# Output projection of a hybrid decoder step: classical blocks against Strassen's seven products

## The chip, the cores and the metric

The kernel runs on one core of one Trainium2 chip. The metric is device time in microseconds (us) for one execution of the whole step; less is better. Three timed runs of the kernel before gave 1225.06, 1226.51 and 1226.95 us. Engines are named as in the profile: PE (matrix multiply), PEld (its weight load), DVE (vector), ACT (scalar), POOL (GpSimd), SP (issues the DMAs).

## The reference

One layer: x <- x + W_out [mLSTM ; GDN], then a final RMSNorm. 1040 prompt tokens (16 meta tokens, whose outputs are dropped, and 1024 real ones) and 8 sample tokens share the weights.

```python
u = _rms_norm(x, norm_w) @ w_in                       # 1048 x 1024 @ 1024 x 8216
ym = (_head_rms(hm).reshape(bsz, t, M_V) * w_mnorm * sigmoid(o_m) * silu(z_m))
yg = (_head_rms(og) * w_gnorm).reshape(bsz, t, G_V) * silu(z_g)
y = jnp.concatenate([ym, yg], axis=-1) @ w_out        # 1032 x 2048 @ 2048 x 1024
x = x + y
y_prompt = _rms_norm(xp[:, META:], final_norm_w)
```

The change concerns the last product, `y @ w_out`, with the residual and the final norm behind it. All data are f32. A product of f32 precision is made of three matmuls in the type fp32r: each operand a is split into a high part h (ACT's copy to fp32r) and a low part l = a - h (a subtraction on DVE), and h*H + l*H + h*L are summed in PSUM.

## The kernel before, in words

**Input projection.** 65 weight tiles of 128 output columns (a gate tile, 24 GDN tiles, 16 mLSTM tiles, 24 gate-path tiles) are multiplied one after another; most are jobs of 72 matmuls (3 token blocks of up to 350 columns, 8 tiles of K, 3 terms). Feature-major: the weight tile stands still, tokens move. A job's raw weights are loaded two jobs ahead by SP into one of two buffers `wr`, split by ACT and DVE during the job before. The recurrences of the 8 GDN heads and the 4 mLSTM heads, and the 8 samples, are woven between these matmuls.

**Gates.** `gate(kt, wcol)` makes one of 16 tiles y (128 features x 1024 tokens): it loads the head output `ht` from DRAM, scales it on POOL, turns it with 8 PE transposes (`hT`), multiplies it with the gate on DVE. kt 8..15 are the GDN half of K, kt 0..7 the mLSTM half. mLSTM gates follow the last 16 jobs (`o0, zm0, ... o7, zm7`) one pair at a time. Of each y the first 256 tokens are split in SBUF, the other 768 are written to DRAM (`y_d`).

**Output projection.** Three token blocks of 256, 512 and 264 columns (`OUT`; the 8 samples ride in the last). For each block, each of 8 output tiles f and each half of K, 24 matmuls (8 K tiles, 3 terms) with the weight tile standing still: 3 x 8 x 2 x 24 = 1152 matmuls. Each half tile of weights (512 KB) is loaded, split and used once per block, so 48 loads. `finish` copies a PSUM tile to SBUF on ACT, turns it back to token-major with PE transposes (`otr`), and adds it to the residual rows `xr` on DVE; squares, mean and scaling follow per block.

**What sets the order.** The kernel is one generator program run by `Plan`, which keeps a clock for each engine and emits instructions thread by thread; `filler` is the thread of the projections, and all others (`chains`, `gates`, `finish`, loads) are stepped in between when the plan thinks their inputs are there. The order in each engine's queue is fixed by this at build time. SP's queue is in order too: a DMA whose wait is not met holds back all behind it.

Of the kernel before, what the change touches and what calls it, by code (L numbers as in the profile page):

```python
# [20 lines left out]
P = 128  # L21
D = 1024
# [42 lines left out]
class Plan:  # L65
# [9 lines left out]
    def __init__(self):  # L75
# [5 lines left out]
        self.threads = []  # L81

    def note(self, eng, op, out, ins, extra, power):
# [4 lines left out]
        if op == "dma_start":  # L88
            load = getattr(out.tensor, "space", DRAM) != DRAM
            start = max([self.clock[eng], self.read.get(out.tensor.name, 0.0), self.dmas[-self.QUEUED]] + [self.done.get(x.tensor.name, (0.0, ""))[0] for x in ins])  # L90
# [7 lines left out]
            self.done[out.tensor.name] = self.dmas[-1], "dma"  # L98
            return
        start = self.clock[eng]  # L100
        for x in ins:
            t, e = self.done.get(x.tensor.name, (0.0, eng))
            if e != eng:
                start = max(start, t + self.LAT)
            elif eng == "pool" or self.place.get(x.tensor.name) == x.offset:
                start = max(start, t + self.SELF[eng])
        for x in (*ins, out):
            t, e = self.last.get(x.tensor.name, (0.0, eng))
            if e != eng:
                start = max(start, t + self.LAT)  # L110
        ptr = sum(free(x) == 1 for x in ins[1:])
        if eng == "pe":
# [7 lines left out]
            else:  # L120
                cost = 1e-3 * m + (0.0 if self.tiled else 0.32)
# [16 lines left out]
        for x in ins:  # L138
            self.read[x.tensor.name] = start + cost
        for x in (*ins, out):  # L140
            if x.tensor.name in self.psum:
                self.last[x.tensor.name] = start + cost, eng
        for x in (out, extra):
            if x is not None:
                self.done[x.tensor.name] = start + cost, eng
                self.place[x.tensor.name] = x.offset

    def shares(self, op, out, ins):

        if any(x.tensor.name in self.psum for x in (*ins, out)):  # L150
# [3 lines left out]
    def when(self, x, wait):  # L154
        t, e = self.done.get(x.tensor.name, (0.0, ""))
        return t + (self.DMA if e == "dma" else wait + self.POOL * (e == "pool"))

    def take(self, tag, bufs, t):

        names, name = self.banks.setdefault(tag, [""] * bufs), t.tensor.name  # L160
# [21 lines left out]
    def step(self, t):  # L182
# [5 lines left out]
        if isinstance(x, tuple):  # L188
            t[1] = self.done.get(x[0].tensor.name, (0.0, ""))[0] + x[1]
# [1736 lines left out]
```

## Time and profile before

| | |
|---|---|
| three runs, median (range) | 1226.51 us (1225.06 to 1226.95) |
| the profiled execution, its own time | 1225.61 us |
| its span in the trace | 1223.8 us |
| PE busy | 1208.6 us, 99% |
| DVE, ACT, POOL busy | 794.1, 584.9, 498.9 us |
| output projection on PE, first to last matmul | 1025.3 to 1214.2 us |
| last matmul to the end of the span | 9.6 us |

All instructions go through a recording helper, so every one carries line 56; they are told apart by the tiles they write and read. `op` is the output projection's PSUM tile, `pjzm` that of the last input projection. Matmul durations in the trace overlap (they are pipelined), so a matmul's price is read from the distance between starts.

### The profile page before, as it was taken

What the parts mean: (1) busy time and instruction counts of PE and PEld (TensorE: products, weight loads), DVE (VectorE), ACT (ScalarE), POOL (GpSimd) and SP (SyncE); (2) the same over time, 40 slices, a digit from 0 to 9 for tenths busy, and PEclk for the clock granted to TensorE, in tenths of its full rate; (3) what the DMA queues carried; (4) which work ended last, traced back from release to release, by engine and by line L of the source; (5) the groups of instructions that cost most, each with busy time, mean ns of one, the idle gap of its engine ahead of it and who ended that gap; (6) DMA issues with size and microseconds to landing.
All of it is one profiled execution on the core that took longest, in us unless ns stands there. A gap on an engine that the chain in (4) does not pass through costs nothing.

```text
span 1223.8 us, 23909 instructions
## 1 busy us (share of the span) xinstructions
PE 1208.6 (99%) x8802; PEld 1150.5 (94%) x8802; DVE 794.1 (65%) x2053; ACT 584.9 (48%) x1861; POOL 498.9 (41%) x674
## 2 busy tenths in 40 slices
PE   9999999999999999999999999999999999999997
PEld 7999999999999999999998999999999999988896
DVE  6789786687968688953356556457567644763365
ACT  6544355667465656554544435342222223644344
POOL 3105887818584837682030431434365310000001
PEclk9999999999999999999999999999999999999998
DMA  6032213221312221212132353335687535793362
GB/s 238 18 99 84 79 43 87 81 72 41 87 54 64 66 78 47 67 61 56 31 99 91 136 167 119 130 141 178 234 292 271 185 141 206 257 327 103 97 217 85
DMA packets 83312, 150.80 MB, mean 123 GB/s; under 512 B 26089, under 2 KB 49857, under 8 KB 83194
## 3 DMA queue, kind: packets, MB, share of 16 engines
q1 hardware_dynamic: 83000, 149.10, 36.8%
q8 instruction: 69, 1.13, 0.4%
q14 instruction: 49, 0.40, 0.1%
q10 hardware_dynamic: 194, 0.17, 0.1%
HBM read 113.97 MB, written 35.26 MB: 122 GB/s over the span
## 4 chain that ended last, share of the span: by engine, by line
PE 88%; DVE 6%; issue 4%; ACT 1%; POOL 1%; DVEq 0%; POOLq 0%; ACTq 0%
PE pjg L56 20%; PE op L56 14%; PE pjm L56 12%; PE pjz L56 7%; PE pjzm L56 7%; PE pjo L56 7%; PE up L56 4%; PE tp L56 3%; PE sk L56 2%; PE mnm L56 2%; PE mup L56 1%; PE hT L56 1%; PE kk L56 1%; PE E L56 1%; PE W L56 1%
## 5 line engine op out<-in xcount | busy, mean ns | idle before, releaser
L56 PE MATMUL pjg<-xht,whg 128*128 128x350 f32 (+6 forms) x624 | 197.7, 324 | 1.0 <-ACT xht L56 1.0
L56 PE MATMUL pjg<-xlt,whg 128*128 128x350 f32 (+6 forms) x624 | 197.1, 323 | 0.0
L56 PE MATMUL pjg<-xht,wlg 128*128 128x350 f32 (+6 forms) x592 | 191.2, 326 | 0.0
L56 POOL TENSOR_TENSOR tmp<-B,E 33x31 f32<-33x31 f32 (+15 forms) x248 | 146.8, 592 | 74.8 <-DMA B<-nd 56.0
L56 PE MATMUL op<-y,who 128*128 128x256 f32 (+2 forms) x768 | 173.3, 319 | 0.0
L56 POOL TENSOR_TENSOR E<-E,tmp 33x31 f32<-33x31 f32 (+15 forms) x248 | 155.4, 627 | 19.4
L56 PEld LDWEIGHTS op<-y,who 128*128 128x128 f32 x768 | 126.9, 188 | 9.5
L56 PE MATMUL pjm<-xht,whm 128*128 128x350 f32 (+2 forms) x384 | 126.6, 330 | 0.0
L56 PE MATMUL pjm<-xht,wlm 128*128 128x350 f32 (+2 forms) x384 | 126.4, 329 | 0.0
L56 PE MATMUL pjm<-xlt,whm 128*128 128x350 f32 (+2 forms) x384 | 125.9, 328 | 0.0
L56 PE MATMUL op<-y,wlo 128*128 128x256 f32 (+2 forms) x384 | 124.3, 324 | 0.1
L56 PEld LDWEIGHTS pjg<-xht,whg 128*128 128x128 f32 x624 | 116.5, 189 | 1.8 <-issue 1.2
L56 PEld LDWEIGHTS pjg<-xlt,whg 128*128 128x128 f32 x624 | 116.4, 189 | 0.5
L56 PEld LDWEIGHTS pjg<-xht,wlg 128*128 128x128 f32 x592 | 111.0, 189 | 0.4
L56 DVE SCALAR_TENSOR_TENSOR kq<-cr,prm,kq 128x346 f32<-128x346 f32 (+7 forms) x147 | 92.5, 633 | 11.5 <-ACT cr L56 5.4
L56 PEld LDWEIGHTS op<-y,wlo 128*128 128x128 f32 x384 | 72.2, 188 | 5.2 <-DVE wlo L56 0.3
L56 PEld LDWEIGHTS pjm<-xht,wlm 128*128 128x128 f32 x384 | 72.5, 189 | 1.0 <-issue 0.4
L56 PEld LDWEIGHTS pjm<-xht,whm 128*128 128x128 f32 x384 | 72.4, 188 | 0.6 <-issue 0.4
L56 PEld LDWEIGHTS pjm<-xlt,whm 128*128 128x128 f32 x384 | 72.3, 188 | 0.3 <-issue 0.2
L56 DVE TENSOR_TENSOR wlo<-wro,who 128x384 fp32r<-128x384 f32 (+1 forms) x90 | 41.5, 508 | 36.8 <-ACT who L56 36.8
L56 PE MATMUL pjz<-xlt,whz 128*128 128x344 f32 x192 | 62.8, 327 | 0.0
L56 POOL TENSOR_TENSOR fst<-fst,mhalf 128x1 f32<-128x1 f32 (+1 forms) x9 | 5.0, 580 | 141.5 <-DVE fst L56 141.5
(319 smaller groups left out, 3171.9 us busy)
## 6 DMA issues: line engine op xcount, KB each, us to landing
wrg<-in_wt SPq DMA_DIRECT2D x23, 512.0 KB
ebuf<-in_wo SPq DMA_DIRECT2D x22, 512.0 KB
wro<-in_wo SPq DMA_DIRECT2D x22, 512.0 KB
wrm<-in_wt SPq DMA_DIRECT2D x16, 512.0 KB
ht<-h_d SPq DMA_DIRECT2D x16, 512.0 KB
y_d<-y SPq DMA_DIRECT2D x16, 384.0 KB
yr<-y_d SPq DMA_DIRECT2D x12, 512.0 KB
gm<-rows_d SPq DMA_DIRECT2D x8, 576.0 KB
```

What stands on the lines that cost most here:

```text
L56: r = f(*args, **kw)
```

## The change

The output projection is computed as Strassen's product of 2 x 2 blocks. The left matrix y is cut into token halves (512 tokens) and K halves (GDN first, mLSTM second); W_out into the same K halves and two halves of 512 output columns. Seven block products (`PRODUCTS`) take the place of eight; each is 4 token tiles x 8 K tiles x 3 terms = 96 matmuls of 512 columns, 672 in all. Now the token tile stands still (128 x 128 of the left block) and 512 weight columns move, so the result is token-major and is added to the residual rows directly from PSUM (`drain`), without copy and without transposes.

- **Left blocks.** The first product's left block (GDN, first tokens) is split in SBUF by the gates (`slot`). Second-half minus first-half (`s_d`), the mLSTM second half and four sums or differences (`c_d`) are formed by POOL in the gates and written to DRAM: 1 subtraction of 512 per GDN gate, an addition of 1024 and two operations of 512 per mLSTM gate, which also reads the GDN tile back from `y_d`. For products 1..6 each of the 8 left tiles is loaded over its own used low part (`left_loads`), and split by ACT and DVE (`left_splits`).
- **Right blocks.** The 16 raw weight pieces (2 K tiles x 512 columns, 512 KB) are loaded once and stay: in `ebuf`, in `wr`, and in 12 places of the memory of x, which is free when the input projection has ended (`places`, `weight_loads`). Five products need a sum or difference of two pieces: 20 POOL operations of 128 x 1024 (`right_sums`). 28 right operands are split into two buffers in turn (`right_splits`): operand n needs the matmuls of operand n - 2 done.
- **Samples.** 32 f32 matmuls against the raw weights: 32 columns (8 samples and neighbours) stand still, in four column groups of the array in turn, 512 weight columns move (`sample_rows`).
- Square sums and scaling are taken per token tile, when the last product that touches a half row has been drained.

PE's order where the last input job ends, before (`pjzm` <- `xht`, `xlt`: last job; `who`, `wlo`: high and low part of a weight tile; `hT`: the last gate):

```order
L56 MATMUL pjzm_2_12936<-xlt,whzm_12813 128x344
L56 MATMUL pjzm_2_12936<-xht,wlzm_12814 128x344
L56 MATMUL op_0_12975<-y_8_10675,who_0_1_12909 128x256 x2
L56 MATMUL op_0_12975<-y_8_10675,wlo_0_1_12910 128x256
...
L56 MATMUL op_0_12975<-y_12_11745,who_0_1_12909 128x256 x2
L56 MATMUL hT_0_13004<-ident,ht_12760 128x128 x4
L56 MATMUL hT_1_13010<-ident,ht_12760 128x128 x4
```

and in the change (`owh`, `owl`: a right operand; `left`: high and low left tiles; `op_0` to `op_3`: the four token tiles):

```order
L56 MATMUL pjzm_2_12986<-xlt,whzm_12837 128x344
L56 MATMUL pjzm_2_12986<-xht,wlzm_12838 128x344
L56 MATMUL op_0_13031<-owh_12914,left_10758 128x512
L56 MATMUL op_0_13031<-owl_12915,left_10758 128x512
L56 MATMUL op_0_13031<-owh_12914,left_10758 128x512
L56 MATMUL op_1_13032<-owh_12914,left_10758 128x512
L56 MATMUL op_1_13032<-owl_12915,left_10758 128x512
L56 MATMUL op_1_13032<-owh_12914,left_10758 128x512
L56 MATMUL hT_0_13041<-ident,ht_12880 128x128 x4
L56 MATMUL hT_1_13047<-ident,ht_12880 128x128 x4
```

Both start the output projection right behind the last job, with the last gate's eight transposes inside.

SP's queue from the moment the memory of x is free, in the change (`regionxh`, `regionxl`: weight pieces in the memory of x; `left<-s_d`: left tiles of product 1; `yg`, `c_d`: the last mLSTM gate; `in_x_p`: residual rows):

```order
L56 DMA regionxh<-in_wo 128x1024 x5
L56 DMA left_10758<-s_d 128x512
L56 DMA c_d<-y_12960 128x512
L56 DMA yg_13066<-y_d 128x1024
L56 DMA left_10758<-s_d 128x512
L56 DMA regionxh<-in_wo 128x1024
...
L56 DMA xr_3_13217<-in_x_p 128x1024
L56 DMA xr_3_13219<-in_x_p 128x1024
L56 DMA db<-in_final_w 128x1024
L56 DMA regionxl<-in_wo 128x1024
L56 DMA left_10758<-c_d 128x512 x2
```

From the first row to the last `regionxl<-in_wo` shown stand 30 DMAs: 9 weight pieces, 8 left tiles, 8 residual tiles, the final norm's weights, and 4 of the last gate, 12.75 MiB; that last piece is the first that product 2 needs. Before, the weight loads were spread over the whole projection.

POOL's queue at the same place (`db`, `regionxl` on the left: sums of weight pieces; `ht`, `yg`: left sums of the last two mLSTM gates):

```order
L56 TENSOR_TENSOR db<-wout_12763,wout_12871 128x1024
L56 TENSOR_TENSOR ht_12880<-ht_12880,rs_12882 128x1024
L56 TENSOR_TENSOR ht_12811<-y_12879,yg_12932 128x1024
L56 TENSOR_TENSOR yg_12932<-yg_12932,y_12879 128x512
L56 TENSOR_TENSOR yg_12932<-y_12879 128x512
L56 TENSOR_SCALAR gs<-mg_12920,wmq 128x8
L56 TENSOR_TENSOR regionxl<-regionxh 128x1024 x2
L56 TENSOR_TENSOR regionxl<-regionxh,ebuf_101 128x1024
L56 TENSOR_TENSOR ht_12880<-y_12960,yg_13066 128x1024
```

Before, POOL had only the `ht`, `gs` and `rs` work of the gates here, and nothing but the norms' small operations behind it.

The diff, cut to what the prediction speaks of (left out: the plan's bookkeeping by parts of a tile, the rings' choice of any free buffer, the residual loads, the old loads of y):

```diff
         pool.tensor_scalar(gs[:, kt_, :], g[:, SEQ:NO], wcol, None, op0=ALU.mult)
+        (r_v if kt_ < 8 else r_gm).free(gi)
+        u = ht.rearrange("p c t -> p (c t)")
+        yield y
+        if kt_ >= 8:
+            sp.dma_start(y_d[j], y)
+            high, low = slot(j)
+            act.copy(high, y[:, 0:HALF])
+            pool.tensor_tensor(out=u[:, 0:HALF], in0=y[:, HALF:SEQ], in1=y[:, 0:HALF], op=ALU.subtract)
+            yield high
+            dve.tensor_tensor(out=low, in0=y[:, 0:HALF], in1=high.bitcast(F32), op=ALU.subtract)
+            yield u
+            sp.dma_start(s_d[j], u[:, 0:HALF])
+        else:
+            sp.dma_start(c_d[j, :, 0], y[:, HALF:SEQ])
+            yield r_gm.can
+            gi, g = r_gm.get([SEQ], f"yg{j}")
+            sp.dma_start(g, y_d[j])
+            yield g
+            pool.tensor_tensor(out=u, in0=y, in1=g, op=ALU.add)
+            yield u
+            sp.dma_start(c_d[j, :, 1:3], u.rearrange("p (a t) -> p a t", a=2))
+            pool.tensor_tensor(out=g[:, 0:HALF], in0=g[:, 0:HALF], in1=y[:, HALF:SEQ], op=ALU.add)
+            pool.tensor_tensor(out=g[:, HALF:SEQ], in0=y[:, 0:HALF], in1=y[:, HALF:SEQ], op=ALU.subtract)
+            yield g
+            sp.dma_start(c_d[j, :, 3:5], g.rearrange("p (a t) -> p a t", a=2))
+            r_gm.free(gi)
         r_gm.free(hi)
-        (r_v if kt_ < 8 else r_gm).free(gi)
-        yield y
-        yh_, yl_ = y0[kt_]
-        act.copy(yh_, y[:, 0:NB])
-        yield yh_
-        dve.tensor_tensor(out=yl_, in0=y[:, 0:NB], in1=yh_.bitcast(F32), op=ALU.subtract)
-        yield y
-        sp.dma_start(y_d[kt_], y[:, NB:SEQ])
         r_y.free(yi)
         done.add(("y", kt_))
...
+    PRODUCTS = (
+        (((0, 1), (1, 1), SUB), ((0, 1, ADD), (1, 1, ADD))),
+        (((0, 0), (0, 1), ADD), ((1, 1, ADD),)),
+        (((1, 0), (0, 0), SUB), ((0, 0, ADD), (1, 0, ADD))),
+        (((0, 0), None, None), ((1, 0, ADD), (1, 1, SUB))),
+        (((0, 0), (1, 1), ADD), ((0, 0, ADD), (1, 1, ADD))),
+        (((1, 1), None, None), ((0, 0, SUB), (0, 1, ADD))),
+        (((1, 0), (1, 1), ADD), ((0, 0, ADD),)),
+    )
+    LEFT = (None, (s_d, None), (c_d, 0), (c_d, 2), (c_d, 3), (c_d, 1), (c_d, 4))
+    NP, NI = len(PRODUCTS), 4
...
+    def places():
+
+        yield has("samples")
+        for e in ebuf:
+            yield e.rearrange("p a b -> p (a b)")
+        for i in range(2):
+            yield has("split", i)
+            t = wp.tile([P, 2 * HALF], F32, tag="wr", name=f"wout{i}")
+            plan.read[t.tensor.name] = plan.read.get(wrs[-2], 0.0)
+            wrs.append(t.tensor.name)
+            yield t
         yield has("x")
+        for tag, old in (("xh", xht), ("xl", xlt)):
+            t = xp.tile([P, 32 * 264], F32, tag=tag, name=f"region{tag}")
+            plan.split(t, D, old.tensor.name)
+            region.extend(t[:, D * i : D * i + D] for i in range(8))
+        done.add(("region",))
+        yield from region[0:12]
...
+    def weight_loads():
+
+        where = places()
+        for q in [((r, 1), i) for i in range(NI) for r in range(2)] + [((r, 0), i) for r in range(2) for i in range(NI)]:
+            for t in where:
+                if hasattr(t, "tensor"):
+                    break
+                yield t
+            (r, c), i = q
+            if c == 0:
+                yield has("used", r, 2 * i)
+            raw[q] = t.rearrange("p (k c) -> p k c", k=2)
+            sp.dma_start(raw[q], a["wo"][r, c, i])
+            if len(raw) % 2 == 0:
+                yield None
+        done.add(("raw",))
+
+    def right_sums():
+
+        n = 0
+        for p, ((b1, b2, op), _) in enumerate(PRODUCTS):
+            for i in range(NI):
+                yield lambda: (b1, i) in raw and (b2 is None or (b2, i) in raw)
+                t = raw[b1, i]
+                if b2 is not None:
+                    yield lambda: all(m in right for m in sums if m < n - 1) and (n != 1 or 0 in right)
+                    if n > 1:
+                        yield has("region")
+                    yield raw[b1, i]
+                    yield raw[b2, i]
+                    t = (fwb if n < 2 else region[12 + n % 2]).rearrange("p (k c) -> p k c", k=2)
+                    pool.tensor_tensor(out=t, in0=raw[b1, i], in1=raw[b2, i], op=op)
+                sums[n] = t
+                n += 1
+
+    def right_splits():
+
+        for n in range(NP * NI):
+            yield lambda: n in sums and ("item", n - 2) in done
+            yield sums[n]
+            wh, wl = (wp.tile([P, 2, HALF], F32R, tag=f"w{i}", name=f"ow{i}{n}") for i in "hl")
+            if n > 1:
+                plan.old.update((x.tensor.name, plan.read[o.tensor.name] + plan.LAT) for x, o in zip((wh, wl), right[n - 2]))
+            for k in range(2):
+                act.copy(wh[:, k], sums[n][:, k])
+            for k in range(2):
+                dve.tensor_tensor(out=wl[:, k], in0=sums[n][:, k], in1=wh[:, k].bitcast(F32), op=ALU.subtract)
+            right[n] = wh, wl
+
+    def left_loads():
+        for p in range(1, NP):
+            t, c = LEFT[p]
             for k in range(8):
+                yield lambda: ("used", p - 1, k) in done and (p == 1 or ("y", k) in done)
+                sp.dma_start(slots[k][1].bitcast(F32), t[k] if c is None else t[k, :, c])
+                done.add(("left", p, k))
+
+    def left_splits():
+
+        for p in range(1, NP):
+            for k in range(8):
+                yield has("left", p, k)
+                high, low = slots[k]
+                yield low
+                yield "act"
+                act.copy(high, low.bitcast(F32))
+                yield high
+                yield "dve"
+                dve.tensor_tensor(out=low, in0=low.bitcast(F32), in1=high.bitcast(F32), op=ALU.subtract)
+                done.add(("parts", p, k))
+
+    def out_products():
+
+        for p in range(NP):
+            banks = []
+            for tag in ("pj", "pj", "k", "k") if p % 2 == 0 else "ssss":
+                yield room(tag)
+                banks.append(bank(tag, f"op{p}_{len(banks)}"))
+            done.add(("product", p))
+            steps = [(k, t) for i in range(NI - 1) for k in (2 * i, 2 * i + 1) for t in range(4)] + [(k, t) for t in range(4) for k in (6, 7)]
+            if p == NP - 1:
+                steps = steps[0:16] + [(k, t) for k0 in (4, 6) for t in (0, 1) for k in (k0, k0 + 1)] + [(k, t) for t in (2, 3) for k in range(4, 8)]
+            for k, t in steps:
+                n = NI * p + k // 2
+                yield lambda: n in right
+                wh, wl = right[n]
+                yield wl
+                yield has("parts", p, k) if p else lambda: ("y", 8 + k) in done
+                yield slots[k][1]
+                for x, (l, r) in enumerate(((0, wh), (0, wl), (1, wh))):
+                    pe.matmul(banks[t], slots[k][l][:, P * t : P * t + P], r[:, k % 2], start=k == 0 and x == 0, stop=k == 7 and x == 2)
+                if t == 3:
+                    done.add(("used", p, k))
+                    if k % 2:
+                        done.add(("item", n))
+                if k == 7:
+                    plan.add(drain(p, t, banks[t]))
+                yield None
...
+    def drain(p, t, pt):
+
+        to = PRODUCTS[p][1]
+        yield lambda: all((c, t) in xr for c, _, _ in to) and (p == 0 or ("drain", p - 1, t) in done)
+        for c, h, op in to:
+            x_ = xr[c, t][:, HALF * h : HALF * h + HALF]
+            yield x_
+            dve.tensor_tensor(out=x_, in0=x_, in1=pt, op=op)
+        done.add(("drain", p, t))
+        if p not in (3, 4, 5, 6):
+            return
+        c, h = {3: (1, 0), 4: (1, 1), 5: (0, 1), 6: (0, 0)}[p]
+        x_, last = xr[c, t], p in (4, 6)
+        part = x_[:, HALF * h : HALF * h + HALF]
+        if not last:
+            stats[c, t] = w("fst", [4], f"fst{c}_{t}", 9)
+        st = stats[c, t]
+        yield part
+        act.activation(junk, part, AF.Square, accum_out=st[:, last : last + 1])
+        if not last:
+            yield st
+            dve.tensor_scalar(st[:, 0:1], st[:, 0:1], EPS * D, None, op0=ADD)
+            if p == 5:
+                yield lambda: ("fw",) in done
+                pool.tensor_tensor(out=part, in0=part, in1=fwb[:, HALF * h : HALF * h + HALF], op=ALU.mult)
+            return
+        yield st
+        dve.tensor_scalar(st[:, 2:3], st[:, 1:2], st[:, 0:1], 1.0 / D, op0=ADD, op1=ALU.mult)
+        pool.tensor_tensor(out=st[:, 3:4], in0=st[:, 2:3], in1=mhalf[:, 0:1], op=ALU.pow)
+        yield st
+        if p == 4:
+            yield lambda: ("fw",) in done
+            yield "dve"
+            dve.scalar_tensor_tensor(out=x_, in0=x_, scalar=st[:, 3:4], in1=fwb, op0=ALU.mult, op1=ALU.mult)
+        else:
+            dve.scalar_tensor_tensor(out=part, in0=part, scalar=st[:, 3:4], in1=fwb[:, 0:HALF], op0=ALU.mult, op1=ALU.mult)
+            act.activation(x_[:, HALF:D], x_[:, HALF:D], AF.Copy, scale=st[:, 3:4])
+        q0 = HALF * c + P * t
+        sp.dma_start(o["y_p"][q0 : q0 + P, :], x_)
...
+        for h in range(2):
+            yield room("s")
+            pt = pst(f"ops{h}")
+            for k in range(16):
+                j = k % 4
+                pe.matmul(
+                    pt[32 * j : 32 * j + 32], yf[:, 8 * k : 8 * k + 32], raw[(k < 8, h), k % 8 // 2][:, k % 2],
+                    start=k < 4, stop=k >= 12)
...
-    def finish(blk, f, pt):
...
-            act.copy(oT[:, 0:m_], pt[:, c0 : c0 + m_])
-            tr = pst(f"otr{blk}_{f}_{c0}")
-            for i, m in part:
-                j = P * i - c0
-                pe.transpose(tr[0:m, j : j + P], oT[:, j : j + m], ident)
-            for i, m in part:
-                j, x_ = P * i - c0, xr[blk, i][2]
-                dve.tensor_tensor(out=x_[0:m, fs], in0=x_[0:m, fs], in1=tr[0:m, j : j + P], op=ALU.add)
...
-    def out_products():
-
-        for blk in range(3):
-            seq = [(f, half) for f in range(8) for half in (1, 0)]
-            if blk == 0:
-                seq[0:8] = [(f, 1) for f in range(4)] + [(f, 0) for f in range(4)]
-            for f, half in seq:
-                yield blk, f, half
...
-        "wo": w_out.reshape(2, KT, P, 8, P).transpose(3, 0, 2, 1, 4),
+        "wo": w_out.reshape(2, 4, 2, P, 2, D // 2)[::-1].transpose(0, 4, 1, 3, 2, 5),
```

More of the change, by code (lines that the diff above doesn't have):

```diff
@@ L80, in __init__, with key, split @@
         self.banks, self.dmas = {}, [0.0] * self.QUEUED
-        self.threads = []
+        self.threads, self.parts, self.old = [], {}, {}
+    def key(self, x):
+        name = x.tensor.name
+        if name not in self.parts:
+            return name
+        pitch, size = self.parts[name]
+        return name, x.offset % pitch // size
+    def split(self, t, size, old=None):
+        pitch = t.ap[0][0] if old is not None else 1 << 40
+        self.parts[t.tensor.name] = pitch, size
+        if old:
+            for i in range(pitch // size + 1):
+                self.read[t.tensor.name, i] = self.read.get(old, 0.0)
     def note(self, eng, op, out, ins, extra, power):
@@ new lines, in hymba_kernel, with slot @@
+    s_d = dr.tile([GH, P, HALF], F32, name="s_d")
+    c_d = dr.tile([GH, P, 5, HALF], F32, name="c_d")
+    for t, size in ((y_d, P * SEQ), (s_d, P * HALF), (c_d, 5 * P * HALF)):
+        plan.split(t, size)
+    slots = {}
+    r_y = Ring(plan, lambda i, name: wk.tile([P, SEQ], F32, tag="BE"[i], name=name, bufs=1), 2)
+    def slot(k):
+        if k not in slots:
+            r, n = (r_kq, 2) if k < 6 else (r_N, 1)
+            _, t = r.get([n, 2, HALF], f"left{k}", F32R)
+            plan.split(t, HALF, r.old)
+            for i in range(n):
+                slots[k + i] = t[:, i, 0], t[:, i, 1]
+        return slots[k]
@@ new lines, in hymba_kernel, with residual @@
+    stats = {}
+    def residual():
+        yield has("region")
+        xs_ = region[15][0:NS]
+        for n, (c, t) in enumerate([(c, t) for t in range(4) for c in range(2)]):
+            if c == 0:
+                yield has("used", 0, 4 + t)
+            if n == 0:
+                x_ = region[14]
+            else:
+                r = r_v if n < 5 else r_gm
+                yield lambda: r.can() and (n < 5 or ("y", 7) in done)
+                _, x_ = r.get([D], f"xr{c}_{t}")
+            q0 = HALF * c + P * t
+            sp.dma_start(x_, a["x_p"][q0 : q0 + P, :])
+            xr[c, t] = x_
+        yield lambda: 1 in right
+        sp.dma_start(fwb, a["final_w"].partition_broadcast(P))
+        done.add(("fw",))
+        yield has("raw")
+        sp.dma_start(xs_, a["x_s"])
+        xr["s"] = xs_
```

313 lines of the change are left out of this document (80 added, 233 removed).

## The prediction

> **What bounds the kernel now.** First the page: busy time by engine, the slices, the chain.
>
> ```profile
> PE 1208.6 (99%) x8802; PEld 1150.5 (94%) x8802; DVE 794.1 (65%) x2053; ACT 584.9 (48%) x1861; POOL 498.9 (41%) x674
> ...
> PE   9999999999999999999999999999999999999997
> ...
> PEclk9999999999999999999999999999999999999998
> ...
> PE 88%; DVE 6%; issue 4%; ACT 1%; POOL 1%; DVEq 0%; POOLq 0%; ACTq 0%
> ```
>
> PE has work in every slice but the last, at full granted clock, and is 88% of the chain that ended last. Time is saved only by taking work off PE, or in the tail; everything else counts once it makes PE wait. Next the stretches of the output projection (its three blocks, then the tail; columns: PE, PEld, DVE, ACT, POOL busy us, clock, DMA share, GB/s):
>
> ```profile
> 1025.30:1068.60 43.30, 43.30 (x370) 43.30 (x369) 29.85 (x65) 26.78 (x63) 0.93 (x1) 1.00 0.87 310
> 1068.60:1166.50 97.90, 97.90 (x476) 81.72 (x476) 45.72 (x119) 41.49 (x108) 1.10 (x2) 1.00 0.48 167
> 1166.50:1213.90 47.40, 47.31 (x389) 46.73 (x388) 31.44 (x80) 24.53 (x69) 4.75 (x6) 1.00 0.49 167
> 1213.90:1223.80 9.90, 0.87 (x6) 0.37 (x4) 5.26 (x12) 2.63 (x8) 3.32 (x4) 0.67 0.29 110
> ```
>
> PE is gapless in all three blocks; DVE reaches 69% and POOL is nearly idle. So a cheaper product is worth its full PE time, as long as DVE, POOL and the DMAs keep up.
>
> **What leaves PE, and what comes.** The timeline of PE (start, us, operation; x2: two merged):
>
> ```profile
> 1025.33 0.40 PE L56 MATMUL op<-y,who 128*128 128x256 f32 x2
> ...
> 1027.68 1.04 PE L56 MATMUL hT<-ident,ht 128*128 128x128 f32 x8
> 1028.47 0.37 PE L56 MATMUL op<-y,wlo 128*128 128x256 f32 x1
> ...
> 1102.32 0.62 PE L56 MATMUL op<-y,who 128*128 128x512 f32 x2
> ...
> 1107.76 0.62 PE L56 MATMUL op<-y,who 128*128 128x512 f32 x2
> ...
> 1213.94 0.28 PE L56 MATMUL op<-y,wlo 128*128 128x264 f32 x1
> ```
>
> The old projection takes 1213.94 + 0.28 - 1025.33 = 188.9 us, with its narrow blocks, 72 transposes back and the last gate's hT. A matmul of 512 columns: 24 stand between 1102.32 and 1107.76, 0.2267 us each, at clock 1.00 over the whole middle block. The change has the same shape (128 x 128 stands still, 512 columns of fp32r move): 672 x 0.2267 = 152.3 us. The hT stay: 1028.47 - 1027.68 = 0.8.
>
> The 32 sample matmuls are new. Nearest rows: eight f32 matmuls in four column groups with 128 columns, and single f32 matmuls with 257 columns:
>
> ```profile
> 865.52 0.65 PE L56 MATMUL mqc<-db,msam 128*32 128x128 f32 x16
> 866.10 0.42 PE L56 MATMUL pjzm<-xht,whzm 128*128 128x344 f32 x1
> ...
> 701.66 0.60 PE L56 MATMUL mnm<-C,mwq 128*128 128x257 f32 x2
> 702.10 0.60 PE L56 MATMUL mnm<-va,mpm 128*128 128x257 f32 x2
> ```
>
> A single one costs 0.44 for 257 columns, so 0.88 for 512; 32 one after another 28 us. The eight took 0.58, 0.0725 each, where one alone would be 0.44 / 2 = 0.22: three at a time. By that row 32 x 4 x 0.0725 = 9.3 us; with all four groups busy 28 / 4 = 7. I take 8, between these, since longer streams lose less at the change of groups.
>
> PE: -188.9 + 152.3 + 0.8 + 8 = **-27.8 us**.
>
> **What PE may have to wait for in the steady products.** A block of 24 matmuls (one right operand) lasts 24 x 0.2267 = 5.44 us, a product 21.8. Prices:
>
> ```profile
> L56 DVE TENSOR_TENSOR wlo<-wro,who 128x384 fp32r<-128x384 f32 x44 | 22.6, 554 | 33.6 <-ACT who L56 33.6
> L56 ACT CAST who<-wro 128x384 fp32r<-128x384 f32 x44 | 20.4, 513 | 16.5 <-PE op L56 13.1 <-issue 3.4
> L56 DVE TENSOR_TENSOR y<-yr,y 128x1024 fp32r<-128x1024 f32 x12 | 14.6, 1220 | 3.1 <-ACT y L56 3.1
> L56 ACT CAST y<-yr 128x1024 fp32r<-128x1024 f32 x12 | 12.5, 1046 | 1.2 <-DMA yr<-y_d 1.2
> L56 DVE SCALAR_TENSOR_TENSOR y<-hT,wmq,mg 128x512 f32<-128x512 f32 x2 | 1.4, 747 | 0.0
> L56 POOL TENSOR_TENSOR ebuf<-ebuf,wb 128x1024 f32<-128x1024 f32 x8 | 15.2, 1898 | 23.2 <-DMA ebuf<-mvb_d 23.2
> ```
>
> By interpolation to 512 columns a DVE split is 0.69 and an ACT copy 0.62; a drain from PSUM is at most the 0.75 of the `y<-hT` row; a POOL sum of 1024 is 1.9. A right operand may be split once operand n - 2 has been used, so one block before its own use: ACT 0.62, then DVE 0.69 for the first half, 2 x 0.62 + 0.69 = 1.9 for both, in 5.44. The left tiles have three quarters of a product, 16 us, for load, copy and split. DVE per product: 8 x 0.69 right, 8 x 0.69 left, 8 x 0.75 drains = 17.0 of 21.8 us, 78%; ACT 16 x 0.62 = 9.9; POOL 4 x 1.9 = 7.6. All fit under PE's 21.8; if this cover goes, see the rivals. Bounds for these waits: 0, and 14 (rival A). I take 1, near the zero end, because PE stayed gapless with DVE at 69% in these very blocks.
>
> **What PE may wait for at the start.** Two rows for a load of 512 KB (issued, and first used by POOL), two for the lead of the last jobs' weights:
>
> ```profile
> 977.28 0.33 SPq L56 DMA_DIRECT2D wro<-in_wt  x1
> 1000.64 0.42 SPq L56 DMA_DIRECT2D ht<-h_d  x1
> ...
> 1005.31 1.90 POOL L56 TENSOR_TENSOR ht<-ht,rs 128x1024 f32<-128x1024 f32 x1 [1.27 <-DMA ht<-h_d]
> ...
> 1005.42 8.80 PE pjo L56 x56
> ```
>
> A load is there after 4.7 us; 0.52 MB at the 310 GB/s of the first block are 1.7 of it, so 3.0 is latency. At full DMA share the rate would be 310 / 0.87 = 356. Product 0's third operand needs the first two pieces loaded into x: 4.7 + 1.7, POOL 1.9, ACT 0.62: 8.9 us after x is free, needed after two blocks, 10.9. It holds by 2. Product 2's first operand is tighter: its piece is the last of 12.75 MiB (13.4 MB) in SP's queue. At 310 it lands after 43.1 + 3.0, at 356 after 37.6 + 3.0; with POOL and ACT 48.6 or 43.1. Product 2 begins 2 x 21.8 + 0.8 = 44.3 us after the first. Wait between 0 and 4.3; I take 2. Ahead of that piece in SP's queue stand residual loads and left tiles that wait for PE's use of the old ones; behind it product 2's left tiles.
>
> **Gate stage.** POOL gets 8 x 1.2 + 8 x (1.9 + 2 x 1.2) = 44 us (512 columns at 1.2, between half and two thirds of the 1.9), DMA some 14.7 MB more. Cover:
>
> ```profile
> 800.00:900.00 100.00, 98.76 (x680) 93.55 (x680) 57.57 (x149) 31.73 (x96) 42.15 (x27) 1.00 0.59 198
> 900.00:950.00 50.00, 50.00 (x380) 48.09 (x379) 36.27 (x57) 13.35 (x36) 31.37 (x19) 1.00 0.80 278
> 950.00:1000.00 50.00, 50.00 (x342) 49.49 (x340) 29.19 (x63) 11.35 (x28) 15.31 (x11) 1.00 0.48 162
> 1000.00:1025.00 25.00, 25.00 (x164) 24.98 (x163) 7.75 (x16) 5.29 (x13) 2.21 (x2) 1.00 0.26 83
> ```
>
> POOL is busy 91 of 225 us here, 135 after. The DMAs move 43.9 MB, 58.6 after: 260 GB/s of 356. SP's queue now has DMAs that wait for POOL, ahead of weight loads; but these are issued at 977.28 for a job at 1005.42, 28 us ahead. I count 0; from that cover, a weight load would have to be 15 us late before PE feels it.
>
> **Tail.**
>
> ```profile
> 1211.24 4.16 POOL L56 TENSOR_TENSOR xr<-xr,db 128x896 f32<-128x896 f32 x2 [39.62 <-issue]
> 1211.79 1.58 DVE L56 TENSOR_TENSOR fst<-fst 128x1 f32<-128x1 f32 x1 [0.30 <-ACT wa L56]
> 1213.48 1.94 DVE L56 TENSOR_TENSOR fst<-fst 8x1 f32<-8x1 f32 x1
> 1216.61 1.82 POOL L56 TENSOR_TENSOR fst<-fst,mhalf 128x1 f32<-128x1 f32 x3 [1.20 <-DVE fst L56]
> ...
> 1219.86 0.30 SPq L56 DMA_DIRECT2D out_y_s<-xr  x1
> ...
> L56 ACT ACTIVATE wa<-xr 128x512 f32<-128x512 f32 x8 | 5.1, 632 | 0.8 <-DVE xr L56 0.6
> L56 DVE TENSOR_TENSOR fst<-fst 128x1 f32<-128x1 f32 x8 | 2.7, 333 | 1.1 <-ACT wa L56 1.1
> ```
>
> Now 5.6 us pass from the last matmul to the last output's issue, with copy, transposes, three squares and three powers. After: drain 0.75, square 0.8 (512 columns on ACT, 0.63, and its read-out, put at 0.2), a small DVE step 0.2, power 0.6, scaling 0.7, handovers put at 0.5: 3.5. But the last output is 512 KB instead of 32 KB, 1.4 us at 356. Gain 0 to 2; I take 1.
>
> **Sum.** 1225.6 (the profiled execution) - 27.8 - 1 + 1 + 2 = 1199.8. The median stands 0.9 above that execution: **1201 us**.
>
> **Rivals.**
> *A, DVE becomes the bound by POOL's lock.* In the last fence two DVE additions of single numbers took 1.58 and 1.94 us while POOL ran its two of 2 us; the other seven of the group's eight take (2.7 - 1.58) / 7 = 0.16. So a long POOL operation can hold DVE for its length. If each of the 20 sums does that to a split, a product costs DVE 17.0 + 7.6 = 24.6 against 21.8, +2.8 in five products: 1201 - 1 + 14 = 1214. Against: a third of DVE's time here reads PSUM. (The Trainium skill, page "SBUF — State Buffer", section "SBUF: two separate sides", says that DVE and GpSimd share one port pair under an exclusive lock for a whole instruction, for DVE operations with two SBUF inputs; the row above agrees. By that rule alone the sum would be 1214.)
> *B, the loads at the start.* If SP's waits keep the DMAs below 300 GB/s, at 250 the piece lands after 53.6 + 3 + 2.5: 15 us late. Price 6 to 15 in place of 2: 1205 to 1214.
> *C, slower.* The two-buffer chain of right operands becomes the period: if after operand n - 2's last use DVE first finishes a left pair (1.4), two drains (1.5) and waits out a sum (1.9) before the split (1.9), the chain is 6.7, 1.3 over the block; in all 28 blocks +36: 1201 - 1 + 36 = 1236. It decides from 26 / 28 = 0.95 us of excess per block. Against: that is the whole DVE load of a block, and two operands are in flight.
> *D, the gates.* SP's waits for POOL hold up weight loads; at 1 us per job of the last 16, 1217. For: SP waits in order; against: 28 us of lead.
> That the products are not really fewer is excluded: the order holds 672.
>
> **How the numbers follow.** Forecast 0.62, with its own range 1195 (no wait, samples 7, tail 2) to 1206; A 0.10; B 0.15; C 0.05; D 0.05; the rest 0.03 is faster still. The range of 8 in 10 takes in A, B and D: 1194 to 1217. A measurement of this kernel tells 0.2% (2.5 us) from no change; faster by more than that are all but C, and 0.02 for a mixture of A, B and D that just cancels the gain: 0.93; same 0.02; slower 0.05.
>
> **What would show it.** Right: `op` matmuls 0.227 us apart over some 163 us, PE gapless but for a few us around product 2; no `otr`. Wrong: PE waiting for `owl` or `owh` in every block (A, C), for DMA pieces in products 0 to 2 (B), PE gaps before 1025 (D), or sample matmuls taking 28 us.

## The result, and the profile after

The change made the kernel slower: 1241.56 us median of 4 runs (1237.19 to 1244.01) against 1226.73 for the kernel before (1225.06 to 1227.1), a ratio of 1.012 with a 95% interval of 1.0085 to 1.0154. The forecast was 1201, its range 1194 to 1217. The profiled execution took 1244.01 us, its span is 1241.9.

The page of the changed kernel, busy time, two rows of the slices, and the chain by engine and by line:

```profile
PE 1197.3 (96%) x8314; PEld 1115.5 (90%) x8314; DVE 858.0 (69%) x1964; ACT 560.9 (45%) x1750; POOL 608.5 (49%) x728
...
PE   9999999999999999999999999999898888999996
...
PEclk9999999999999999999999999999899988999999
...
PE 73%; DVE 9%; DMA 8%; issue 5%; POOL 3%; ACT 1%; SPq 1%; POOLq 0%; DVEq 0%; ACTq 0%
PE pjg L56 20%; PE pjm L56 12%; PE op L56 9%; PE pjz L56 7%; PE up L56 4%; PE pjzm L56 4%; PE tp L56 3%; PE pjo L56 3%; DMA c_d<-yg 3%; PE sk L56 2%; DMA ht<-h_d 2%; DVE left L56 2%; PE mnm L56 1%; POOL ht L56 1%; PE mup L56 1%
```

Before, PE was 88% of the chain and no DMA stood in it. Now DMAs are 8% of it, and two are named: the write of `c_d` out of `yg`, and the load of `ht`. PE has holes in five of the slices from 29 to 34, and in three of these five its clock is lower too. Slice 29 begins at 869 us: that is the gate stage, not the projection. The stretches show how much (columns as in the prediction; the stage from 800 us to the first `op` matmul, the projection, the tail), first the kernel before, then the change:

```profile
800.00:1025.30 225.30, 224.06 (x1561) 216.42 (x1561) 130.78 (x282) 61.71 (x173) 91.04 (x58) 1.00 0.58 195
```

```profile
800.00:1059.70 259.70, 234.88 (x1560) 224.82 (x1559) 156.03 (x274) 60.95 (x165) 140.54 (x89) 0.95 0.65 217
...
1059.70:1234.00 174.30, 167.35 (x746) 129.32 (x745) 147.39 (x186) 69.54 (x139) 66.98 (x34) 0.99 0.47 164
1234.00:1242.00 8.00, 0.41 (x2) 0.00 (x0) 2.44 (x5) 2.14 (x4) 1.54 (x2) 0.83 0.64 256
```

Much the same 1560 matmuls take 34.4 us longer before the projection begins. Of these PE is idle for 24.8 - 1.2 = 23.6 (stretch less busy time, of each kernel), and busy for 234.9 - 224.1 = 10.8 more, at a mean clock of 0.95. The projection itself became shorter: from the first `op` matmul at 1059.7 to the end of the last at 1234.4 are 174.7 us, 14.2 less than the 188.9 before. The tail is 7.5 in place of 9.6. Together +34.4 - 14.2 - 2.1 = +18.1, and the two profiled executions differ by 18.4. So the projection's gain is there, if only 14.2 us of the 24.8 forecast (27.8 less 3 of waits), and the gate stage gives back more than all of it.

Who waits in the stage from 800 to 1062, in the groups of waits of the change (total us, times, longest):

```profile
POOL ht L56 <- DMA ht<-h_d: 52.2, 11, 10.3
...
PE hT L56 <- POOL ht L56: 18.0, 7, 5.2
```

These waits for `ht` are 18.0 of PE's 24.8 us of idle time; the largest of the rest are 3.0 for DVE's `wb` and 2.1 for a load of the samples' state. What SP's queue waits for there:

```profile
SPq L56 <- DMA c_d<-yg: 35.6, 6, 7.4
SPq L56 <- DMA s_d<-ht: 34.0, 8, 5.8
SPq L56 <- DVE y L56: 26.7, 8, 7.6
...
SPq L56 <- POOL ht L56: 12.2, 6, 7.5
```

A piece of the chain of waits shows one round of it (start, us, what):

```profile
945.23 7.54 DMA c_d<-yg
...
953.15 5.44 DMA ht<-h_d
...
958.74 1.91 POOL ht L56
...
960.69 0.67 PE hT L56 x4
...
961.39 1.42 DVE y L56 x2
...
962.86 5.47 DMA yg<-y_d
...
968.40 3.00 POOL ht L56
...
971.46 3.71 POOL yg L56 x2
...
978.81 7.87 DMA c_d<-yg
```

A gate's sums are written to DRAM for 7.5 us; only then may the next GDN gate's `gg` be loaded, since it goes into the buffer that the write reads (`r_gm` has three, and `gg`, `ht` and now `yg` all come from it). Its `ht`, which goes into the buffer of the write `c_d<-ht` issued just before, stands behind `gg` in SP's queue. After the load come POOL's scaling, the transposes on PE, `y`, the reading back of the GDN tile into the buffer that `gg` held, the sums, 3.6 us of other work on POOL and SP, and the next write: 33.6 us from one `c_d<-yg` to the next. In the same way the mLSTM gate's `ht` waits for the write `s_d<-ht`. Before the change the buffers came free when PE, DVE and POOL had read them, with no DRAM write in between. PE takes its work in order and meets the transposes (`hT`) before POOL has made `ht`. Other than by the forecast's rival D, no weight load is late: the waits of PE hold none for `who`, `wlo`, `whzm` or `wlzm`.

### The profile page after: what moved, and what is told of

The parts are those of the page before. It is cut to its first block, busy times and chain, and to the rows that moved or that the text cites. A ratio compares the mean times of both kernels' runs of the same rounds, so it can differ in the third digit from the quotient of the medians.

```text
span 1241.9 us, 22839 instructions
## 1 busy us (share of the span) xinstructions
PE 1197.3 (96%) x8314; PEld 1115.5 (90%) x8314; DVE 858.0 (69%) x1964; ACT 560.9 (45%) x1750; POOL 608.5 (49%) x728
## 4 chain that ended last, share of the span: by engine, by line
PE 73%; DVE 9%; DMA 8%; issue 5%; POOL 3%; ACT 1%; SPq 1%; POOLq 0%; DVEq 0%; ACTq 0%
PE pjg L56 20%; PE pjm L56 12%; PE op L56 9%; PE pjz L56 7%; PE up L56 4%; PE pjzm L56 4%; PE tp L56 3%; PE pjo L56 3%; DMA c_d<-yg 3%; PE sk L56 2%; DMA ht<-h_d 2%; DVE left L56 2%; PE mnm L56 1%; POOL ht L56 1%; PE mup L56 1%
## 5 line engine op out<-in xcount | busy, mean ns | idle before, releaser
L56 PE MATMUL op<-owh,left 128*128 128x512 f32 x448 | 142.7, 398 | 1.0 <-DVE left L56 0.6
L56 PEld LDWEIGHTS op<-owh,left 128*128 128x128 f32 x448 | 84.7, 189 | 23.1 <-issue 1.7
L56 PE MATMUL op<-owl,left 128*128 128x512 f32 x224 | 89.4, 399 | 5.9 <-DVE owl L56 5.9
L56 POOL TENSOR_TENSOR mwq<-mt,mgm 128x384 f32<-128x384 f32 x12 | 11.3, 940 | 110.1 <-DVE mgm L56 110.1
L56 POOL TENSOR_TENSOR kap<-kap,phalf 128x9 f32<-128x9 f32 x8 | 14.7, 1837 | 101.8 <-DVE kap L56 101.8
L56 PE MATMUL pjo<-xht,who 128*128 128x344 f32 x192 | 63.2, 329 | 1.1 <-DVE mg L56 1.1
L56 PE MATMUL pjo<-xlt,who 128*128 128x344 f32 x192 | 63.7, 332 | 0.0
```

The costliest lines, as they stand in the source:

```text
L56: r = f(*args, **kw)
```

## The experiments

**The buffer of `yg`.** Theory 1: the gates hold each other up through the three buffers. Theory 2: POOL's sums, and SP waiting for POOL. Theory 3: the added bytes. The first run takes only the sharing away; the planner then also finds another order. The tag `tmp` was last used by the GDN inverses.

```diff
+    r_t = Ring(plan, lambda i, shape, name: wk.tile([P] + shape, F32, tag="tmp", name=name, bufs=1), 1)
...
-            yield r_gm.can
-            gi, g = r_gm.get([SEQ], f"yg{j}")
+            yield r_t.can
+            gi, g = r_t.get([SEQ], f"yg{j}")
...
-            r_gm.free(gi)
+            r_t.free(gi)
```

> The tile into which a gate reads y back (yg) gets a buffer of its own, one that has been idle since the GDN inverses, and no longer takes one of the three that gg and ht also need. Nothing else changes; the work and its bytes are the same. Theory 1 (buffers): the changed kernel's projection starts 34 us late because the next gate's load of ht waits on SP until the write of c_d out of the buffer it is to go into has landed (35.6 us in 6 waits in its trace); then these waits go, the first op matmul comes at 1030 to 1040 in place of 1059.7, and the time is 1212 to 1222. Theory 2 (the gates' 44 us of sums on POOL, and SP that waits for POOL ahead of other transfers): nothing of that is changed here, the first op matmul stays above 1052 and the time at 1235 or more. Theory 3 (the added bytes): as theory 2.

Measured: 1212.28 us median (1210.23 to 1214.34, 4 runs), a ratio of 0.9885 to the kernel before (0.9866 to 0.9904). The first `op` row of its tile's view, its wait of PE for `ht`, and the stage:

```profile
L56 PE MATMUL op<-owh,left x448: 387/394/501, 1031.8 to 1200.7; 128*128 128x512 f32 x150
```

```profile
PE hT L56 <- POOL ht L56: 4.2, 3, 1.5
```

```profile
800.00:1031.80 231.80, 225.50 (x1567) 216.99 (x1566) 150.87 (x274) 61.13 (x166) 143.88 (x89) 1.00 0.71 247
```

Theory 1 said 1212 to 1222 and 1030 to 1040, and holds; theories 2 and 3 said nothing would move. All sums and all bytes are still there: POOL is as busy as in the change (143.9 us), and DMA moves them faster, 247 GB/s. 27.9 of the 34.4 us are gone, and the kernel is now faster than the one before.

**Sums and writes taken away.** Three more runs leave out the writes, the sums, or both, with the three shared buffers kept. The first line below goes, with the other three sums of the gates, in `g_none` and `g_writes_only`; the rest, with the other three writes, in `g_none` and `g_sums_only`.

```diff
-            pool.tensor_tensor(out=u, in0=y, in1=g, op=ALU.add)
...
-            sp.dma_start(c_d[j, :, 1:3], u.rearrange("p (a t) -> p a t", a=2))
...
-                sp.dma_start(slots[k][1].bitcast(F32), t[k] if c is None else t[k, :, c])
+                sp.dma_start(slots[k][1].bitcast(F32), y_d[k, :, 0:HALF])
```

> Leaves out the gates' sums on POOL and the writes of s_d and c_d; products 1 to 6 read the first half of y in their place, so the output is another. y_d is still written and read back. All three theories: the gate stage is as before, the first op matmul at 1025 to 1032, and the time at 1205 to 1212. If the first op matmul stays above 1040, all three fall, and the order in which the hT transposes are put among PE's other work, or the reading back, is what costs.

> The gates' sums are formed on POOL, but not written to s_d and c_d; products 1 to 6 read the first half of y in their place, so the output is another. Theory 1 (buffers held until a write has landed): the buffers come free when POOL is done, so the first op matmul comes at 1027 to 1036 and the time at 1205 to 1216. Theory 2 (POOL's work and who waits for it): most of the 34 us stays, first op matmul 1046 or later, time 1226 or more. Theory 3 (bytes): as theory 1.

> The gates' sums are left out, but the tiles are written to s_d and c_d as if they had been formed, so the output is another; products 1 to 6 read them. Theory 1 (buffers held until a write has landed): most of the 34 us stays, since every write still has to land before its buffer is loaded again; without POOL's 4 to 6 us per gate in the chain, the first op matmul comes at 1042 to 1055 and the time at 1222 to 1238. Theory 2 (POOL): the loss is gone, first op matmul at 1025 to 1034, time 1205 to 1214. Theory 3 (bytes): as the changed kernel, 1055 or later.

Measured, the stage up to the first `op` matmul, without both (1205.31 us), sums only (1222.78) and writes only (1224.91), one run each:

```profile
800.00:1027.80 227.80, 224.62 (x1564) 216.74 (x1563) 133.29 (x274) 61.35 (x165) 93.38 (x60) 1.00 0.58 201
```

```profile
800.00:1044.20 244.20, 230.19 (x1565) 221.83 (x1564) 158.97 (x274) 61.30 (x165) 144.40 (x89) 0.97 0.55 188
```

```profile
800.00:1047.70 247.70, 233.77 (x1586) 224.68 (x1585) 129.46 (x278) 62.09 (x168) 90.06 (x60) 0.98 0.71 234
```

Without both the loss is gone, as all theories said. Writes only come 19.9 us later than that, in the range of theory 1 and against theories 2 and 3. In that run, though, PE is behind already at 800 us: its first matmul of the last 16 jobs (`pjo`) starts at 806.5, in the run with neither at 802.8. From there to the first `op` matmul the writes cost 16.2 us. Sums only lose 16.4 (16.3 counted from `pjo`), where theory 1 said 0 to 8, and the 1044.2 lies just short of theory 2's 1046: that miss stands. So it is not the landing alone. The sums can hold the buffers too, from the load of `ht` to the last sum. And there is a second path: in that run PE waits 5.5 us once for DVE's `wb`, and DVE is busy for 159.0 us against 129.5 without sums, with the same 274 to 278 instructions. For `ht` it waits 5.8 us there. Which share each path has in the 16.4 is open. What the run with the buffer apart adds is that sums and writes together, unshared, cost only 4.0 us over the run with neither (1031.8 against 1027.8).

**The order.** The planner that sets the order of all queues took a tile as free when its write was issued. Told that the write must land first, it puts other loads and other PE work ahead:

```diff
             self.done[self.key(out)] = self.dmas[-1], "dma"
+            for x in ins:
+                if out.tensor.name[0:3] in ("y_d", "s_d", "c_d"):
+                    self.read[self.key(x)] = self.dmas[-1]
             return
```

> The changed kernel, with one rule added to the planner: a tile that is being written to y_d, s_d or c_d counts as read until that write has landed, where the planner took it as free when the write was issued. The work and the buffers are the same, only the order may change: SP and PE are given other work ahead of the loads that have to wait. Theory 1 (the gates hold each other up through three buffers, so that their chain is too long): other work fills some of PE's gaps, but the last gates still come late; first op matmul at 1050 to 1060 and 1232 to 1243 us. Rival (the chain is short enough, only the order in which PE meets the hT transposes is wrong): first op matmul below 1040, time below 1222.

Measured: 1227.13 us (1224.03 to 1230.4, 6 runs), ratio 1.0007 (0.999 to 1.0023); the first `op` matmul comes at 1048.0. PE still waits for `ht` eight times, but briefly:

```profile
PE hT L56 <- POOL ht L56: 13.1, 8, 2.5
```

The time lies 5 us better than theory 1 had it and 5 us worse than the rival: a third of the gate stage's loss (1059.7 - 1048.0 = 11.7 us), and 14.4 us of the time, was the order, made without knowledge of the landing; the larger part stays with the shared buffers. With `yg` in its own buffer the same rule gives the very same program, so that run already has the better order: of its 27.9 us, 11.7 are the order and 1048.0 - 1031.8 = 16.2 the buffer.

**SP's queue.** On top of the buffer apart, the five writes (of `y_d`, `s_d` and three of `c_d`) are issued by POOL:

```diff
-            sp.dma_start(s_d[j], u[:, 0:HALF])
+            pool.dma_start(s_d[j], u[:, 0:HALF])
```

> As the run in which yg has a buffer of its own (1212.3 us, first op matmul 1031.8), and besides the writes to y_d, s_d and c_d are issued from POOL's queue instead of SP's, so that no load stands behind a write that waits for POOL or DVE. If what is left of the gate stage (6.5 us later than before) is SP held up by those writes (24.4 us behind DVE y, 22 behind POOL ht and yg in that run): first op matmul 1026 to 1029, time 1206 to 1210. If it is not SP: 1030 to 1034 and 1210 to 1215; if issuing costs POOL time that the sums need, later than that, 1215 or more.

Measured: 1220.47 us (1215.77 to 1222.62, 6 runs), ratio 0.9946 (0.9928 to 0.9965), first `op` matmul at 1043.5: worse by 8 us than with the writes on SP. That is the number of the last of the three expectations, but not its reason: POOL is not late, as PE's waits for `ht` below show. One of DVE's groups from 800 to 1031, with the writes on SP and on POOL:

```profile
L56 DVE TENSOR_TENSOR wlzm<-wrzm,whzm 128x384 fp32r<-128x384 f32 (+1 forms) x24 | 17.1, 744 | 2.8 <-ACT whzm L56 2.8
```

```profile
L56 DVE TENSOR_TENSOR wlzm<-wrzm,whzm 128x384 fp32r<-128x384 f32 (+1 forms) x24 | 36.9, 1570 | 2.4 <-ACT whzm L56 2.4
```

and PE's waits in the run with the writes on POOL:

```profile
PE pjzm L56 <- DVE wlzm L56: 5.5, 1, 5.5
...
PE hT L56 <- POOL ht L56: 0.7, 1, 0.7
```

A free SP does help the gates: PE's waits for `ht` fall from 4.2 to 0.7 us. But DVE's weight splits take twice as long, and PE waits 5.5 us for one of them, 2.5 for DVE's `wb` and 2.6 for a load. Two places of DVE and POOL in that run show which work of POOL the slow splits stand beside:

```profile
942.81 0.58 POOL L56 DMA_DIRECT2D s_d<-ht  x1 [0.41 <-POOL ht L56]
942.88 0.41 DVE L56 TENSOR_TENSOR wlzm<-wrzm,whzm 128x256 fp32r<-128x256 f32 x1
...
997.80 11.73 DVE L56 TENSOR_TENSOR wlzm<-wrzm,whzm 128x384 fp32r<-128x384 f32 x3
...
1003.15 2.41 POOL L56 TENSOR_TENSOR ht<-y,yg 128x1024 f32<-128x1024 f32 x1
```

Beside the issuing of a write a split of 256 columns takes its usual 0.41 us. The three that take 11.73 us, the last of which PE waits for, take 1.5 us undisturbed (0.56, 0.55 and 0.42 from 823 us on). They stand beside five of POOL's sums and a scaling, 10.7 us from 998.9 to 1010.7 with two short issues between them. So it is the sums, which now come in one row beside these splits, and not the issuing.

**The projection: POOL's lock.** On top of the buffer apart, POOL's sums of weights are left out, and then given to DVE (these are 20, not the 24 of the two expectations):

```diff
-                    pool.tensor_tensor(out=t, in0=raw[b1, i], in1=raw[b2, i], op=op)
+                    dve.tensor_tensor(out=t, in0=raw[b1, i], in1=raw[b2, i], op=op)
```

> As the run in which yg has a buffer of its own, without POOL's 24 sums of weights: each product uses the first of its two weight pieces as it is, so the output is another. Of the forecast's rivals, the lock of POOL and DVE says that these sums make DVE's splits of owl and left two to three times as long (1232 and 1709 ns in the changed kernel from 1060 to 1120, 682 alone) and that this sets PE's waits: without them both groups have means of 0.68 to 0.75 us, PE's waits in the projection (2.6 us for owl) go to below 0.5, and the time from the first to the last op matmul falls from 169 to 164 to 167. If the waits come from the pieces' transfers instead (1060 to 1080 at 357 GB/s), they stay at 2 us or more, and so does the stage at 168 or more.

> As the run in which yg has a buffer of its own (1212.3 us; DVE's groups for left and owl of 128x512 there at means of 1067 and 910 ns), with the 24 sums of weights formed by DVE in place of POOL. If it is the lock with POOL that makes DVE late, DVE does 24 more instructions of an estimated 1.2 to 1.4 us (twice the 0.68 of one 128x512 of two tiles in that trace), 29 to 34 us, and its splits fall by 48 x 0.3 + 48 x 0.2 = 24 to 31 us: its load is about the same, no split stands still for a whole sum of 2.4 us, PE's waits for owl go from 2.6 to 0 to 2 us, and the time is 1207 to 1212. If DVE's load is what sets PE's waits, not the lock: 1212 to 1217.

Measured without the sums: 1205.23 us (one run), and with the sums on DVE 1207.03 us (1205.63 to 1213.37, 4 runs), ratio 0.9853 (0.9825 to 0.988). DVE's two kinds of split in the projection, and the projection's stretch, with POOL's sums (the kernel of the first experiment):

```profile
L56 DVE TENSOR_TENSOR left<-left 128x512 fp32r<-128x512 f32 x48 | 49.8, 1067 | 1.1 <-ACT left L56 1.1
L56 DVE TENSOR_TENSOR owl<-regionxl,owh 128x512 fp32r<-128x512 f32 x36 | 31.4, 910 | 11.5 <-ACT owh L56 11.5
```

```profile
1031.80:1201.10 169.30, 166.02 (x745) 127.98 (x743) 142.14 (x186) 69.70 (x139) 65.49 (x33) 1.00 0.48 165
```

without sums:

```profile
L56 DVE TENSOR_TENSOR left<-left 128x512 fp32r<-128x512 f32 x48 | 35.5, 774 | 1.4 <-ACT left L56 1.4
```

```profile
1030.90:1195.90 165.00, 164.59 (x745) 128.48 (x744) 115.94 (x186) 69.26 (x139) 19.49 (x15) 1.00 0.50 169
```

and with the sums on DVE:

```profile
L56 DVE TENSOR_TENSOR left<-left 128x512 fp32r<-128x512 f32 x48 | 34.3, 746 | 1.2 <-ACT left L56 1.1
```

```profile
1029.80:1196.40 166.60, 164.72 (x745) 128.30 (x743) 137.41 (x205) 69.39 (x139) 18.49 (x15) 1.00 0.49 168
```

Without POOL's sums a split of `left` falls from 1067 to 774 ns, PE's 2.6 us of waits for `owl` are gone, and the stretch is 165.0 us, as the lock's expectation had it but for the 774 (750 at most). With the sums on DVE the wait is 1.4 us, and the time lies at the lower end of the lock's 1207 to 1212. The transfers of the pieces are the same, so it was not these. With the sums on DVE, DVE has 19 instructions more and yet is busy for 5 us less, since it no longer stands still behind POOL. This is the best time of a kernel that computes the whole step, 19.5 us below the kernel before. Its gain of 5 us over the first experiment rests on two ratios to the kernel before whose intervals overlap (0.9853 and 0.9885), so the traces carry that step more than the times.

All four of the gates' sums moved to DVE as well:

```diff
-            pool.tensor_tensor(out=u, in0=y, in1=g, op=ALU.add)
+            dve.tensor_tensor(out=u, in0=y, in1=g, op=ALU.add)
```

> As the run before it in this list (yg with a buffer of its own, sums of weights on DVE), and the gates' sums on DVE too. POOL had 8 x 1.64, 8 x 2.66, 8 x 1.51 and 8 x 1.46 us of them, 58 us; DVE would need an estimated 8 x (0.68 + 1.36 + 0.68 + 0.68) = 27 us, while DVE's busy time from 800 to the first op matmul, 150.9 us there and 130.8 before the change, would lose the 20 us of the lock. If the lock or POOL's time makes up what is left of the gate stage (first op matmul 1031.8 against 1025.3): 1026 to 1029 and 2 to 6 us less than the run before it. If DVE's queue in order is worse for PE than the lock: first op matmul later than 1032.

Measured: 1209.21 us (1206.44 to 1211.27, 4 runs), ratio 0.9853 (0.9833 to 0.9872), not to be told from the run before it; in its profiled execution the first `op` matmul is later, at 1035.3, and PE waits 7.1 us for `ht`. The stage:

```profile
800.00:1035.40 235.40, 228.09 (x1564) 219.96 (x1563) 166.68 (x305) 60.94 (x165) 87.69 (x58) 0.99 0.71 243
```

The gates' sums take DVE 24.0 us there, and it is busy for 166.7, 11.4 more than in the run before it (155.3), so 12.6 of the lock's 20 us came back, not all. A first `op` matmul later than 1032 was the expectation's sign that the sums in DVE's queue cost PE more than the lock did, and PE's waits for `ht` did rise, from 4.2 to 7.1 us. Whether the lock has a part in what is left of the gate stage's loss, this run does not tell.

## Why the prediction was wrong, step by step

The stage from 800 us to the first `op` matmul in seven of the kernels, worked out from stretches like those above (idle: stretch less PE's busy time; longer: PE's busy time over the 224.1 of the kernel before; with the writes only, 25 matmuls of the stage before fall behind 800 us, an estimated 3.9 of the 9.7 at 0.157 us each):

| kernel | first `op` | PE idle | PE busy longer |
|---|---|---|---|
| before | 1025.3 | 1.2 | - |
| the change | 1059.7 | 24.8 | 10.8 |
| planner told of the landing | 1048.0 | 16.3 | 7.6 |
| writes only | 1047.7 | 13.9 | 9.7 |
| sums only | 1044.2 | 14.0 | 6.1 |
| `yg` in its own buffer | 1031.8 | 6.3 | 1.4 |
| neither sums nor writes | 1027.8 | 3.2 | 0.6 |

- **Gate stage, "I count 0; from that cover, a weight load would have to be 15 us late before PE feels it": this step failed, by 34.4 us.** It counted POOL's time (forecast 44 us more; measured 140.5 - 91.0 = 49.5 at the first `op`, with one gate's sums still to come), the bytes, and the lead of one kind of transfer, the weights. It did not ask what the buffers hold. The new writes read `ht` and `yg`, the old `y_d` write read a tile of another ring; so the loads of `gg` and `ht`, with some 4.7 us from issue to use, now start after a write's 7.5. With the order made blind to this it cost 34.4 us, with the better order 22.7, and 6.5 once `yg` had its own buffer. The weight loads with their 28 us of lead were indeed never late.
- **Rival D** named the place and the in-order queue, not the transfer: it expected late weights at 1 us per job, 1217. What SP held up apart from the buffers was worth 3.5 us of waits for `ht` (4.2 to 0.7) in the run with the writes on POOL's queue.
- **-188.9 + 152.3 on PE**: right. Three stretches of the change's projection:

```profile
1080.00:1100.00 20.00, 16.19 (x63) 12.68 (x62) 19.97 (x19) 4.63 (x9) 12.03 (x6) 0.91 0.93 357
1100.00:1120.00 20.00, 19.38 (x90) 14.58 (x92) 19.17 (x20) 8.73 (x17) 9.87 (x4) 1.00 0.56 192
...
1140.00:1160.00 20.00, 20.00 (x88) 16.18 (x87) 16.50 (x26) 7.88 (x15) 0.69 (x1) 1.00 0.32 95
```

  In the quiet one 88 matmuls take 20 us, 0.2273 each against the 0.2267 forecast. Without POOL's sums the stretch from the first `op` matmul to the end of the last is 165.0 us, where the terms 152.3 + 0.8 + 8 + 1 + 2 give 164.1.
- **Samples, 8 in bounds of 7 to 9.3**: the chain of the change has them as two pieces, at 1118.95 and 1123.41, of 3.57 us each: 7.1.
- **Waits in steady products, 1, and at the start, 2**: too small. In the change PE is idle for 7.0 us in the projection, and its clock drops once there. With `yg` in its own buffer the cause is shown: **rival A**, whose mechanism is right and whose price (14) is too high, 169.3 against 165.0 without POOL's sums, 4.3 us; PE waits for `owl` four times only. In the change itself the stretch is longer still (174.7). There the last gate's sums and left tiles fall on the first products: DVE is busy for 20.0 and 19.2 of each 20 us from 1080 to 1120 (rows above), PE for 16.2 of the first, and the chain runs over one load `left<-s_d` of 8.6 us and three splits of 2.1 us each. How these share the 5.4 us was not taken apart.
- **Rival B** falls: POOL waits for pieces of weights, but with `yg` apart PE's waits go away with the transfers unchanged, and from 1080 to 1100 the DMAs move 357 GB/s in the change, not 250. **Rival C** falls: PE waits for `owl` four times in the change, not in every block.
- **Tail, -1 in 0 to -2**: measured 7.5 - 9.6 = -2.1.

The sum without the failed step is close: 1201 was forecast, and the kernels whose gates do not hold each other up give 1212, and 1207 with the sums on DVE.

## What to carry to other kernels

When a tile that was only read by engines becomes the source of a DMA, its buffer is held until that write has landed: count the write's time (7.5 us here) rather than 0 between last use and next load, and follow the ring that the buffer comes from around once, as one chain. A buffer that had been idle since an earlier stage was worth 28 us here, with no operation saved. And when a chain sets the pace, don't only take its links out one at a time: either link alone cost half of the loss, 16 of 32 us, which looked like two causes; uncoupling the chain with both links kept left 4.0 of the 32.

## What the runs showed of the hardware

In the change, idle time of PE cost about half as much again. The stretches around four holes in it (us, PE busy, clock, DMA share, GB/s; PE alone):

```profile
921.00:923.00 2.00, 0.15 (x2) 1.00 0.79 322
923.00:928.00 5.00, 5.00 (x35) 1.00 0.87 315
873.90:878.30 4.40, 0.00 (x0) 0.91 1.02 358
878.30:881.90 3.60, 3.60 (x17) 0.50 0.37 152
881.90:885.30 3.40, 3.40 (x17) 0.65 0.92 260
...
947.00:949.00 2.00, 0.00 (x0) 1.00 0.89 338
...
950.00:951.00 1.00, 1.00 (x7) 0.50 1.04 426
...
1025.30:1030.48 5.18, 0.00 (x1) 0.73 1.00 367
1030.48:1033.90 3.42, 3.42 (x14) 0.50 0.21 86
```

After holes of 4.4 and 5.2 us the granted clock is 0.50 for the next 3.4 us and more; after one of 1.85 us it stays at 1.00. So the change's 23.6 us more of idle time brought 10.8 us of slower matmuls; where no wait of PE was longer than 1.5 us, less (1.4 us with 6.3 of idle time, `yg` in its own buffer). (The Trainium skill, page "TensorE: Matmul & The Clock Gate", section "What's actually happening", says the array falls to half its clock after an idle window of about 3.4 us, and comes back after as long a busy one. The rows agree on the fall; the clock came back 3.5 to 6 us after the hole. By that rule holes below 3.4 us should be free, yet in the same trace one of 2.14 us, before 949.08, was followed by 0.50.)

A write of 512 KB took 7.5 to 7.9 us in the chain from its issue to its landing, with another of 512 KB issued some 0.5 us ahead of it and the DMA share at 0.82 and 0.86 meanwhile. (The Trainium skill, page "DMA: Bandwidth & Descriptors", section "Latency and other measured facts", has a fixed cost of some 2 us for a transfer, most of it the receipt from memory. Estimated from that page, with 436 GB/s, 512 KB would take 3.2 us; the trace has more than twice that here.)

Work of POOL can hold DVE's splits of weights for its length. In the run with the writes on POOL's queue, three of them took 11.73 us beside 10.7 us of POOL's sums and a scaling, while one beside the issuing of a write took 0.41 us.
